# Two of four weight sums by accumulating DMA, and block pairs at the end of a feed-forward group

## The chip, the cores and the metric

The kernel runs on one core of a Trainium2 chip. The metric is the device time of one launch in microseconds; lower is better. TensorE (PE) does matmuls, VectorE (DVE), ScalarE (ACT) and GpSimd (POOL) do elementwise work, SyncE (SP) and GpSimd issue DMAs. Each engine takes its instructions in order, from its own queue.

## The reference

A two-layer encoder over 256 positions with a model width of 2048, in float32. Each layer does:

```
h = rmsnorm(x, norm1_g);  q, k, v, uv = h @ w_in
x = x + concat(rmsnorm(attention(q, k, v)), rmsnorm(gating(uv))) @ w_out
h = rmsnorm(x, norm2_g)
x = x + (silu(h @ w_gate) * (h @ w_up)) @ w_down
```

The change concerns the last two lines: the feed-forward part with w_gate and w_up (2048 x 5632 each), and what stands at its start.

## The kernel before

Every weight matmul is made in a 32-bit reduced type, with both operands split into a high part `hi` and a remainder `lo`; three terms (hi with hi, hi with lo, lo with hi) are summed in PSUM. `split` makes a weight's parts: ScalarE copies the raw weight to `hi` (L858), VectorE subtracts to get `lo` (L859). A raw weight tile, a `hi` and a `lo` of 128x2048 each lie in one of 17 buffers (`Big`, 1 MB). SyncE's queue issues the loads (L830).

The work is a list of groups: projections, out projections (`oa`, `og`), then 11 feed-forward groups a layer, with groups of the down projection between them. In the trace's names, group 9 is the first feed-forward group of layer 0 (here called group 0 of the layer), 10 the next, 11 the third. One feed-forward group makes 512 columns of gate and 512 of up, for both halves of the positions: four PSUM banks v, z (gate and up, first half) and x, w (second half). Its contraction of 2048 rows is eight pairs of 256 rows. Four pairs are done in the ordinary way ("N", two slots of 12 matmuls each: slot one into v and z, slot two into x and w). The other four, the block pairs, go through seven products M1 to M7 in place of eight (a 2x2 block product with seven multiplications), one slot of 12 matmuls each. So a group has 15 slots. The products need sums of weights, which `split` places by `add` (L836) on VectorE: T1 = q11 + q12 after M1's split, T2 = T1 + q22 after M5's (both in q11's buffer), T4 = q21 + T2 after M2's, T3 = q12 + q22 ahead of M3's. They also need sums of the normalized input `h`: `Norm.block` transposes a 512-column block of x (`tpn`), ScalarE scales it to `hr_n`, and `sums` makes seven forms (L252), their `hi` (L255, ACT) and `lo` (L256, DVE), together `h_n`. Ordinary pairs need only `hb_n`, a `hi` and a `lo`.

What sets the order is written by hand: `ORDER` is the order of slots of a group, `FIRST` that of a layer's group 0. Splits are placed two slots ahead of their use (three in group 0), loads five slots ahead; a list of events merges both. Side work (norm blocks, transposes of the feed-forward result `tpf` and its split `ff`) are generators that a scheduler steps through between slots. `finish` takes a bank's result out once its last matmul is done: banks 1 and 5 to 7 are the products' partial results, which it combines (`m1`, `m5`, `m16`, `m5_16`); with v complete `sil` (SiLU on ScalarE, L623) and with z the product with it (L626).

```
ORDER = ("N", "M1", "N", "M5", "M2", "N", "M6", "M3", "M7", "M4", "N")
FIRST = ("M1", "M5", "M2", "M6", "M3", "N", "M7", "N", "M4", "N", "N")
```

Of the kernel before, what the change touches and what calls it, by code (L numbers as in the profile page):

```python
# [14 lines left out]
P = 128  # L15
# [88 lines left out]
def encoder_kernel(ctx: ExitStack, tc: tile.TileContext, x, xf, w, ws, lng, cols, fg, cs, msk, out):  # L104
# [139 lines left out]
    def sums(raw, n, dst):  # L244

        r = raw.view("p (j f q) -> p j f q", j=2, f=8)[:, :n]
        f = lambda i: r[:, :, i, :]
        for to, a, op, b in (
            (3, f(7), ALU.subtract, f(2)), (4, f(3), ALU.subtract, f(0)),
            (5, f(0), ALU.subtract, f(7)), (6, f(1), ALU.add, f(4)),  # L250
        ):
            nc.vector.tensor_tensor(out=f(to), in0=a, in1=b, op=op)  # L252
        src = r[:, :, 0:7, :].rearrange("p j f q -> p j (f q)")
        hi, lo = (dst.rearrange("p (j h z) -> p j h z", h=2, z=7 * P)[:, :, i] for i in range(2))
        nc.scalar.activation(out=hi, in_=src, func=AF.Copy)  # L255
        nc.vector.tensor_tensor(out=lo, in0=src, in1=hi.bitcast(F32), op=ALU.subtract)  # L256
        raw.free()
# [16 lines left out]
    class Norm:  # L274


        def __init__(self, l, which, fast):
            self.l, self.which, self.fast = l, which, fast
            self.ss = smp.tile([P, NT, D // NB], F32, tag="ssn", name=f"ssn_{which}_{l}", bufs=2)
            self.hs = hpool.tile([P, 7 * 2 * KR * P], F32R, tag="h", name=f"h_{which}_{l}")  # L280
            self.pairs, self.bigs = [], []
            at, half = 0, 0
            for p in range(KD // 2):
                if p < fast:
# [4 lines left out]
                if at + 8 * P <= 56 * P:  # L289
# [26 lines left out]
        def block(self, b):  # L316

            fast = [p for p in (2 * b, 2 * b + 1) if p < self.fast]
            raw = Big(f"hr_{self.which}_{self.l}_{b}") if fast else None
            for j in range(2):  # L320
                p = 2 * b + j
                g = [gcol(self.l, self.which, 2 * p + i) for i in range(2)]
                ps = transposes(xt[b], 2 * j, f"tpn_{self.which}_{self.l}_{p}")
                yield 1
                if p < self.fast:
                    r = raw.view("p (j f q) -> p j f q", j=2, f=8)[:, j]
                    nc.scalar.activation(out=r[:, 0:8:7, :], in_=ps[:, 0], func=AF.Copy, scale=g[0])
                    nc.scalar.activation(out=r[:, 1:3, :], in_=ps[:, 1], func=AF.Copy, scale=g[1])
                else:
                    put_splits(self.pairs[p], 0, ps, g)  # L330
                    self.ready[p] = True
                yield 1
            if fast:
                sums(raw, len(fast), self.hs[:, fast[0] * 14 * P:(fast[-1] + 1) * 14 * P])
                for p in fast:
                    self.ready[p] = True
                yield 1
            self.square(b)
# [402 lines left out]
    def done(l, what, idx, t, n, ps):  # L741
# [11 lines left out]
        else:  # L753
# [8 lines left out]
            if what == "og" and t == NT - 1:  # L762
                spawn(norms["n2", l].block(b), delay=1 + n, rank=0)
            if what == last_part:
# [12 lines left out]
    class Group:  # L777


        def __init__(self, g, spec):  # L780
            self.g = g
            self.l, self.what, self.idx, _, self.n, self.fast, _ = spec
            self.banks, self.copies = {}, {}
            rest = iter(range(self.fast, self.n))
            self.slots = []
# [47 lines left out]
        def add(self, to, of):  # L833
            cols = self.fast * NB
            a, b = (self.raw[q].t[:, :cols] for q in (to, of))
            nc.vector.tensor_tensor(out=a, in0=a, in1=b, op=ALU.add)  # L836

        def need(self, key):
            return 1 if isinstance(key, tuple) else 2

        def split(self, key, pieces=1):
# [6 lines left out]
            else:  # L848
# [4 lines left out]
                hi, lo = (z.t[:, :cols] for z in own)  # L853
            if key == "M3":
                self.add("q12", "q22")
            for i in range(pieces):
# [6 lines left out]
            elif key == "M5":  # L863
                self.add("q11", "q22")
            elif key == "M2":
                self.add("q21", "q11")
            elif not (isinstance(key, tuple) and key[1] == 0):
                raw.free()

        def run(self, i):  # L870
# [38 lines left out]
        def finish(self, b):  # L909
            ps, c = self.banks[b][0], self.copies  # L910
            if b in "15":
                c[b] = sx(f"m{b}_{self.g}")
                nc.scalar.activation(out=c[b], in_=ps, func=AF.Copy)
                return
            if b == "6":
# [5 lines left out]
            if b == "7":  # L921
                nc.vector.tensor_tensor(out=c["x"], in0=ps, in1=c["x"], op=ALU.add)
                nc.vector.tensor_tensor(out=c["5"], in0=c["5"], in1=c["x"], op=ALU.subtract)
                c["v"], c["w"] = c["1"], c["5"]
                return
            if b in c:
                nc.vector.tensor_tensor(out=c[b], in0=ps, in1=c[b], op=ALU.add)
                ps = c[b]
            t, n = next(k for k, v in BANK.items() if v == b)
            done(self.l, self.what, self.idx, t, n, ps)  # L930

    groups = [Group(g, spec) for g, spec in enumerate(_groups())]
# [103 lines left out]
def _stream(np, weights):  # L1036

    parts = []
    for l, _, idx, row, pairs, fast, blocks in _groups():
        ab = [weights[name][l, row:row + pairs * 2 * P, c:c + NB].reshape(pairs, 2, P, NB) for name, c in blocks]  # L1040
        z = np.stack(ab, 2)
        rest = iter(z[fast:])
        for m in _order(idx, pairs, fast):
            if m == "N":
                parts.append(next(rest).transpose(2, 0, 1, 3).ravel())
            for q in LOADS.get(m, ()):
                parts.append(z[:fast, int(q[1]) - 1, int(q[2]) - 1].transpose(1, 0, 2).ravel())
    return np.concatenate(parts)
# [54 lines left out]
```

## Time and profile before

| | us |
|---|---|
| median of 3 runs | 2194.11 (2193.1 to 2195.26) |
| the profiled execution | 2191.83 |
| its span in the trace | 2190.0 |
| TensorE busy | 2098.2 (96%) |
| VectorE busy | 1619.8 (74%) |
| ScalarE busy | 1072.1 (49%) |
| GpSimd busy | 79.4 (4%) |

Busy shares are means over the span. Times are those of one core; a row of a timeline gives its start from the span's start, its length, the engine, the line and what it writes and reads, and in brackets how long its engine had been idle and what ended that. Matmul rows overlap, since matmuls are pipelined: their starts, not their lengths, tell how fast they follow each other. "PEclk" in a table of windows is the granted clock of TensorE as a share of its full speed.

### The profile page before, as it was taken

What the parts mean: (1) busy time and instruction counts of PE and PEld (TensorE: products, weight loads), DVE (VectorE), ACT (ScalarE), POOL (GpSimd) and SP (SyncE); (2) the same over time, 40 slices, a digit from 0 to 9 for tenths busy, and PEclk for the clock granted to TensorE, in tenths of its full rate; (3) what the DMA queues carried; (4) which work ended last, traced back from release to release, by engine and by line L of the source; (5) the groups of instructions that cost most, each with busy time, mean ns of one, the idle gap of its engine ahead of it and who ended that gap; (6) DMA issues with size and microseconds to landing.
All of it is one profiled execution on the core that took longest, in us unless ns stands there. A gap on an engine that the chain in (4) does not pass through costs nothing.

```text
span 2190.0 us, 23316 instructions
## 1 busy us (share of the span) xinstructions
PE 2098.2 (96%) x9432; PEld 1720.2 (79%) x9432; DVE 1619.8 (74%) x1432; ACT 1072.1 (49%) x1153; POOL 79.4 (4%) x64
## 2 busy tenths in 40 slices
PE   8999998999999999999999999989999999999997
PEld 7878886778777877877788788867787778778775
DVE  5677668795798589769665776588948976996794
ACT  6446536454355355435453555454544553554453
POOL 0220000000000000000002200000000000000000
PEclk9999998999999999999999999989999999999999
DMA  8444463455444545545544355544454454456452
GB/s 337 183 144 174 173 230 118 165 210 218 187 178 171 213 157 189 200 184 204 200 182 165 135 192 192 192 166 175 160 228 173 160 210 187 173 195 221 177 215 77
DMA packets 58797, 405.81 MB, mean 185 GB/s; under 512 B 6592, under 2 KB 6592, under 8 KB 10560
## 3 DMA queue, kind: packets, MB, share of 16 engines
q1 hardware_dynamic: 58688, 404.31, 49.7%
q8 instruction: 74, 1.21, 0.2%
q14 instruction: 35, 0.29, 0.0%
HBM read 402.19 MB, written 2.10 MB: 185 GB/s over the span
## 4 chain that ended last, share of the span: by engine, by line
PE 80%; DVE 11%; issue 6%; ACT 3%; DMA 0%; SPq 0%; DVEq 0%; POOLq 0%; POOL 0%; ACTq 0%
PE mm_z L880 18%; PE mm_x L880 18%; PE mm_v L880 16%; PE mm_w L880 16%; PE mm L880 8%; DVE lo_M L859 5%; DVE lo L859 2%; ACT hi_M L858 2%; DVE hl L859 1%; PE sp L449 1%; DVE raw_q L836 1%; DVE rb_k L419 0%; PE op L489 0%; PE tpn_n L264 0%; DVE ff L235 0%
## 5 line engine op out<-in xcount | busy, mean ns | idle before, releaser
L859 DVE TENSOR_TENSOR hl<-raw,hl 128x1024 fp32r<-128x1024 f32 (+1 forms) x402 | 479.3, 1240 | 74.4 <-ACT hl L858 72.7
L858 ACT ACTIVATE hl<-raw 128x1024 fp32r<-128x1024 f32 (+1 forms) x402 | 399.9, 1048 | 124.6 <-PE mm_w L880 83.4
L859 DVE TENSOR_TENSOR lo_M<-raw_q,hi_M 128x2048 fp32r<-128x2048 f32 x154 | 350.4, 2286 | 51.0 <-ACT hi_M L858 51.0
L858 ACT ACTIVATE hi_M<-raw_q 128x2048 fp32r<-128x2048 f32 x154 | 288.1, 1909 | 131.3 <-DVE raw_q L836 111.2
L880 PE MATMUL mm<-hi_M,h_n 128*128 128x512 f32 x704 | 236.5, 397 | 1.7 <-DVE h_n L256 1.7
L859 DVE TENSOR_TENSOR lo<-raw,hi 128x2048 fp32r<-128x2048 f32 x88 | 200.7, 2285 | 32.1 <-ACT hi L858 21.9
L836 DVE TENSOR_TENSOR raw_q<-raw_q,raw_q 128x2048 f32<-128x2048 f32 x88 | 201.6, 2290 | 2.3
L858 ACT ACTIVATE hi<-raw 128x2048 fp32r<-128x2048 f32 x88 | 167.6, 1908 | 49.9 <-PE mm_w L880 43.0
L880 PEld LDWEIGHTS mm<-hi_M,h_n 128*128 128x128 f32 x704 | 134.2, 191 | 30.2 <-DVE h_n L256 2.6
L880 PE MATMUL mm_v<-hl,ff 128*128 128x512 f32 x528 | 136.2, 392 | 2.7 <-ACT ff L234 2.7
L880 PE MATMUL mm<-lo_M,h_n 128*128 128x512 f32 x352 | 138.8, 394 | 0.0
L880 PE MATMUL mm_x<-hl,ff 128*128 128x512 f32 x528 | 135.1, 391 | 0.0
L880 PE MATMUL mm_z<-hl,ff 128*128 128x512 f32 x528 | 134.0, 389 | 0.0
L880 PE MATMUL mm_w<-hl,ff 128*128 128x512 f32 x528 | 134.0, 389 | 0.0
L880 PE MATMUL mm_v<-hi,hb_n 128*128 128x512 f32 x352 | 123.3, 391 | 0.0
L880 PE MATMUL mm_z<-hi,hb_n 128*128 128x512 f32 x352 | 122.9, 390 | 0.0
L880 PE MATMUL mm_w<-hi,hb_n 128*128 128x512 f32 x352 | 122.7, 389 | 0.0
L880 PE MATMUL mm_x<-hi,hb_n 128*128 128x512 f32 x352 | 122.6, 389 | 0.0
L880 PE MATMUL mm_v<-hl,h_n 128*128 128x512 f32 x420 | 112.8, 401 | 9.5 <-ACT hl L858 4.8
L880 PEld LDWEIGHTS mm_v<-hl,ff 128*128 128x128 f32 x528 | 98.1, 188 | 25.0 <-ACT ff L234 3.7
L880 PEld LDWEIGHTS mm_z<-hl,ff 128*128 128x128 f32 x528 | 99.1, 188 | 20.7
L880 PEld LDWEIGHTS mm_w<-hl,ff 128*128 128x128 f32 x528 | 99.1, 188 | 20.7
(205 smaller groups left out, 3324.2 us busy)
## 6 DMA issues: line engine op xcount, KB each, us to landing
raw<-in_w SPq DMA_DIRECT2D x287, 1024.0 KB, 4.8
raw_q<-in_w SPq DMA_DIRECT2D x88, 1024.0 KB, 6.6
xt<-in_x SPq DMA_DIRECT2D x4, 512.0 KB, 13.7
out<-xt SPq DMA_DIRECT2D x8, 256.0 KB, 3.1
xf<-in_xf SPq DMA_DIRECT2D x3, 512.0 KB, 10.0
raw<-in_w SPq DMA_DIRECT2D x4, 256.0 KB, 6.3
lw<-in_ws SPq DMA_DIRECT2D x2, 512.0 KB, 5.5
lw<-in_lng SPq DMA_DIRECT2D x2, 512.0 KB, 6.3
```

What stands on the lines that cost most here:

```text
L449: nc.tensor.matmul(sp[:, t, :], lhsT=q[:, a, i, t * P:(t + 1) * P], rhs=k[:, b, i, :], start=(n == 0), stop=(n == len(TERMS) - 1),)
L836: nc.vector.tensor_tensor(out=a, in0=a, in1=b, op=ALU.add)
L858: nc.scalar.activation(out=hi[:, sl], in_=src[:, sl], func=AF.Copy)
L859: nc.vector.tensor_tensor(out=lo[:, sl], in0=src[:, sl], in1=hi[:, sl].bitcast(F32), op=ALU.subtract)
L880: nc.tensor.matmul(bank[0], lhsT=lhsT, rhs=rhs, start=bank[1], stop=stop)
```

## The change

Four edits. First, T3 and T4 are made by an accumulating DMA on GpSimd's queue (`add_dma`: the destination's contents plus the source's), T3 right after M5's split and not ahead of M3's, T4 as before after M2's. There are 22 feed-forward groups, so 44 such transfers, of 1 MB each. Second, the block pairs are the last four of the eight, made from blocks 2 and 3 of x and no longer 0 and 1, and `FIRST` begins with three ordinary pairs. Third, `Norm.block` makes both transposes of a block together, and `sums` leaves a step between the `hi` and the `lo` of the forms; the blocks of the second out projection are spawned later. Fourth, `finish` writes v's result to a tile of its own, `c11`, and holds bank w back until x is done where w's ordinary pairs end before M7, as they do now in group 0.

```
@@ -55,7 +55,7 @@
 
 
 ORDER = ("N", "M1", "N", "M5", "M2", "N", "M6", "M3", "M7", "M4", "N")
-FIRST = ("M1", "M5", "M2", "M6", "M3", "N", "M7", "N", "M4", "N", "N")
+FIRST = ("N", "N", "N", "M1", "N", "M5", "M2", "M6", "M3", "M7", "M4")
 LOADS = {"M1": ("q11", "q12"), "M5": ("q22",), "M2": ("q21",)}
 
 CH = 4 * NB
...
@@ -253,6 +253,7 @@
         src = r[:, :, 0:7, :].rearrange("p j f q -> p j (f q)")
         hi, lo = (dst.rearrange("p (j h z) -> p j h z", h=2, z=7 * P)[:, :, i] for i in range(2))
         nc.scalar.activation(out=hi, in_=src, func=AF.Copy)
+        yield 1
         nc.vector.tensor_tensor(out=lo, in0=src, in1=hi.bitcast(F32), op=ALU.subtract)
         raw.free()
 
...
@@ -315,26 +316,25 @@
 
         def block(self, b):
 
-            fast = [p for p in (2 * b, 2 * b + 1) if p < self.fast]
+            fast = [p for p in (2 * b, 2 * b + 1) if p >= self.slow]
             raw = Big(f"hr_{self.which}_{self.l}_{b}") if fast else None
+            ps = [transposes(xt[b], 2 * j, f"tpn_{self.which}_{self.l}_{2 * b + j}") for j in range(2)]
+            yield 1
             for j in range(2):
                 p = 2 * b + j
                 g = [gcol(self.l, self.which, 2 * p + i) for i in range(2)]
-                ps = transposes(xt[b], 2 * j, f"tpn_{self.which}_{self.l}_{p}")
-                yield 1
-                if p < self.fast:
-                    r = raw.view("p (j f q) -> p j f q", j=2, f=8)[:, j]
-                    nc.scalar.activation(out=r[:, 0:8:7, :], in_=ps[:, 0], func=AF.Copy, scale=g[0])
-                    nc.scalar.activation(out=r[:, 1:3, :], in_=ps[:, 1], func=AF.Copy, scale=g[1])
+                if p >= self.slow:
+                    r = raw.view("p (j f q) -> p j f q", j=2, f=8)[:, j + len(fast) - 2]
+                    nc.scalar.activation(out=r[:, 0:8:7, :], in_=ps[j][:, 0], func=AF.Copy, scale=g[0])
+                    nc.scalar.activation(out=r[:, 1:3, :], in_=ps[j][:, 1], func=AF.Copy, scale=g[1])
                 else:
-                    put_splits(self.pairs[p], 0, ps, g)
+                    put_splits(self.pairs[p], 0, ps[j], g)
                     self.ready[p] = True
-                yield 1
             if fast:
-                sums(raw, len(fast), self.hs[:, fast[0] * 14 * P:(fast[-1] + 1) * 14 * P])
+                yield from sums(raw, len(fast), self.hs[:, (fast[0] - self.slow) * 14 * P:(fast[-1] + 1 - self.slow) * 14 * P])
                 for p in fast:
                     self.ready[p] = True
-                yield 1
+            yield 1
             self.square(b)
 
         def early(self, k, src):
...
@@ -760,7 +760,7 @@
             else:
                 nc.vector.tensor_tensor(out=xb, in0=ps, in1=xb, op=ALU.add)
             if what == "og" and t == NT - 1:
-                spawn(norms["n2", l].block(b), delay=1 + n, rank=0)
+                spawn(norms["n2", l].block(b), delay=1 + n + 2 * idx, rank=0)
             if what == last_part:
                 if l + 1 < DEPTH:
                     if t == NT - 1:
...
@@ -835,6 +836,10 @@
             a, b = (self.raw[q].t[:, :cols] for q in (to, of))
             nc.vector.tensor_tensor(out=a, in0=a, in1=b, op=ALU.add)
 
+        def add_dma(self, to, of):
+            cols = self.fast * NB
+            nc.gpsimd.dma_start(out=self.raw[to].t[:, :cols], in_=self.raw[of].t[:, :cols], accum_op=ALU.add)
+
         def need(self, key):
             return 1 if isinstance(key, tuple) else 2
 
...
@@ -851,8 +856,6 @@
                 src = raw.t[:, :cols]
                 own = [Big(f"{z}_{self.g}_{key}", F32R) for z in ("hi", "lo")]
                 hi, lo = (z.t[:, :cols] for z in own)
-            if key == "M3":
-                self.add("q12", "q22")
             for i in range(pieces):
                 sl = slice(i * cols // pieces, (i + 1) * cols // pieces)
                 nc.scalar.activation(out=hi[:, sl], in_=src[:, sl], func=AF.Copy)
...
@@ -862,8 +865,9 @@
                 self.add("q11", "q12")
             elif key == "M5":
                 self.add("q11", "q22")
+                self.add_dma("q12", "q22")
             elif key == "M2":
-                self.add("q21", "q11")
+                self.add_dma("q21", "q11")
             elif not (isinstance(key, tuple) and key[1] == 0):
                 raw.free()
 
...
@@ -911,6 +915,8 @@
             if b in "15":
                 c[b] = sx(f"m{b}_{self.g}")
                 nc.scalar.activation(out=c[b], in_=ps, func=AF.Copy)
+                if b == "1":
+                    c["v"] = c[b]
                 return
             if b == "6":
                 c["x"] = sx(f"m16_{self.g}")
...
@@ -921,13 +927,19 @@
             if b == "7":
                 nc.vector.tensor_tensor(out=c["x"], in0=ps, in1=c["x"], op=ALU.add)
                 nc.vector.tensor_tensor(out=c["5"], in0=c["5"], in1=c["x"], op=ALU.subtract)
-                c["v"], c["w"] = c["1"], c["5"]
+                c["w"] = c["5"]
+                return
+            if self.fast and b == "w" and "w" not in c:
+                self.held = True
                 return
             if b in c:
-                nc.vector.tensor_tensor(out=c[b], in0=ps, in1=c[b], op=ALU.add)
-                ps = c[b]
+                to = sx(f"c11_{self.g}") if b == "v" else c[b]
+                nc.vector.tensor_tensor(out=to, in0=ps, in1=c[b], op=ALU.add)
+                ps = to
             t, n = next(k for k, v in BANK.items() if v == b)
             done(self.l, self.what, self.idx, t, n, ps)
+            if b == "x" and self.held:
+                self.finish("w")
 
     groups = [Group(g, spec) for g, spec in enumerate(_groups())]
     slots, loads, first_slot = [], [], {}
```

Line numbers move by two to four: the split is at L861 (ACT) and L862 (DVE), `add` at L837, `add_dma` at L841, `finish` between L917 and L937.

On VectorE, in a steady group (11, layer 0), from M5's split on. Before; `raw_11_q21<-raw_11_q21,raw_11_q11` is T4, `lo_11_6` the third ordinary pair's `lo`:

```order
L859 TENSOR_TENSOR lo_11_M5_3317<-raw_11_q11_3202,hi_11_M5_3316 128x2048
L836 TENSOR_TENSOR raw_11_q11_3202<-raw_11_q11_3202,raw_11_q22_3258 128x2048
L859 TENSOR_TENSOR lo_11_M2_3335<-raw_11_q21_3279,hi_11_M2_3334 128x2048
L836 TENSOR_TENSOR raw_11_q21_3279<-raw_11_q21_3279,raw_11_q11_3202 128x2048
L235 TENSOR_TENSOR ff_0_1_3333<-tpf_0_1_0_3351,ff_0_1_3333 128x2x256
L859 TENSOR_TENSOR lo_11_6_3359<-raw_11_6_3299,hi_11_6_3358 128x2048
L235 TENSOR_TENSOR ff_0_1_3333<-tpf_0_1_2_3377,ff_0_1_3333 128x2x256
L859 TENSOR_TENSOR lo_11_M6_3397<-raw_11_q11_3202,hi_11_M6_3396 128x2048
```

Now, where the third ordinary pair is number 2:

```order
L862 TENSOR_TENSOR lo_11_M5_3319<-raw_11_q11_3203,hi_11_M5_3318 128x2048
L837 TENSOR_TENSOR raw_11_q11_3203<-raw_11_q11_3203,raw_11_q22_3260 128x2048
L862 TENSOR_TENSOR lo_11_M2_3338<-raw_11_q21_3281,hi_11_M2_3337 128x2048
L235 TENSOR_TENSOR ff_0_1_3336<-tpf_0_1_0_3354,ff_0_1_3336 128x2x256
L862 TENSOR_TENSOR lo_11_2_3362<-raw_11_2_3301,hi_11_2_3361 128x2048
L235 TENSOR_TENSOR ff_0_1_3336<-tpf_0_1_2_3380,ff_0_1_3336 128x2x256
L862 TENSOR_TENSOR lo_11_M6_3400<-raw_11_q11_3203,hi_11_M6_3399 128x2048
```

T4's row is gone (and T3's, which stood behind `lo_11_M6`), and the third pair's `lo` stands behind the `ff` directly.

On VectorE, where the block operands of a layer's group 0 (group 9) are made. Before, ahead of and beside M1's split:

```order
L252 TENSOR_TENSOR hr_n2_0_0_2483<-hr_n2_0_0_2483 128x2x128 x4
L256 TENSOR_TENSOR h_n2_0_2330<-hr_n2_0_0_2483,h_n2_0_2330 128x2x896
L859 TENSOR_TENSOR lo_9_M1_2592<-raw_9_q11_2538,hi_9_M1_2591 128x2048
L836 TENSOR_TENSOR raw_9_q11_2538<-raw_9_q11_2538,raw_9_q12_2540 128x2048
L252 TENSOR_TENSOR hr_n2_0_1_2513<-hr_n2_0_1_2513 128x2x128 x4
L256 TENSOR_TENSOR h_n2_0_2330<-hr_n2_0_1_2513,h_n2_0_2330 128x2x896
```

Now; `hr_n2_0_2` and `hr_n2_0_3` are blocks 2 and 3:

```order
L862 TENSOR_TENSOR lo_9_2_2664<-raw_9_2_2625,hi_9_2_2663 128x2048
L862 TENSOR_TENSOR lo_9_M1_2707<-raw_9_q11_2659,hi_9_M1_2706 128x2048
L837 TENSOR_TENSOR raw_9_q11_2659<-raw_9_q11_2659,raw_9_q12_2661 128x2048
L252 TENSOR_TENSOR hr_n2_0_2_2695<-hr_n2_0_2_2695 128x2x128 x4
L862 TENSOR_TENSOR lo_9_3_2746<-raw_9_3_2681,hi_9_3_2745 128x2048
L257 TENSOR_TENSOR h_n2_0_2330<-hr_n2_0_2_2695,h_n2_0_2330 128x2x896
L252 TENSOR_TENSOR hr_n2_0_3_2732<-hr_n2_0_3_2732 128x2x128 x4
L257 TENSOR_TENSOR h_n2_0_2330<-hr_n2_0_3_2732,h_n2_0_2330 128x2x896
L862 TENSOR_TENSOR lo_9_M5_2791<-raw_9_q11_2659,hi_9_M5_2790 128x2048
```

The forms of `h` have moved behind M1's split and T1, with the fourth ordinary pair's `lo` (`lo_9_3`) between the two steps of block 2.

On ScalarE, at the end of group 0. Before:

```order
L858 ACTIVATE hi_9_M4_2835<-raw_9_q21_2589 128x2048
L858 ACTIVATE hi_9_6_2856<-raw_9_6_2819 128x2048
L858 ACTIVATE hi_9_7_2886<-raw_9_7_2854 128x2048
L858 ACTIVATE hi_10_4_2932<-raw_10_4_2884 128x2048
L623 ACT_TABLE_LOAD
L623 ACTIVATE sil_0_0_0_2944<-m1_9_2679,rstd_n2_0_2816 128x512
L623 ACTIVATE sil_0_0_1_2961<-m16_9_2756,rstd_n2_0_2816 128x512
L858 ACTIVATE hi_10_M1_2973<-raw_10_q11_2914 128x2048
```

Now:

```order
L861 ACTIVATE hi_9_M3_2853<-raw_9_q22_2743 128x2048
L917 ACTIVATE m5_9_2870<-mm_9_5_2857 128x512
L861 ACTIVATE hi_9_M7_2874<-raw_9_q12_2661 128x2048
L623 ACT_TABLE_LOAD
L623 ACTIVATE sil_0_0_0_2893<-c11_9_2890,rstd_n2_0_2817 128x512
L861 ACTIVATE hi_9_M4_2895<-raw_9_q21_2771 128x2048
L861 ACTIVATE hi_10_0_2936<-raw_10_0_2872 128x2048
L623 ACTIVATE sil_0_0_1_2968<-m16_9_2912,rstd_n2_0_2817 128x512
L861 ACTIVATE hi_10_M1_2974<-raw_10_q11_2916 128x2048
```

The SiLU of the first half, which reads `c11`, has moved ahead of `hi` of M4, and its table load with it.

## Rows read from the trace of the kernel before

**Rows 1.** The page: busy time by engine, and the chain that ended last by engine.
```profile
PE 2098.2 (96%) x9432; PEld 1720.2 (79%) x9432; DVE 1619.8 (74%) x1432; ACT 1072.1 (49%) x1153; POOL 79.4 (4%) x64
...
PE 80%; DVE 11%; issue 6%; ACT 3%; DMA 0%; SPq 0%; DVEq 0%; POOLq 0%; POOL 0%; ACTq 0%
```

**Rows 2.** Waits of TensorE: us in total, times, longest.
```profile
PE mm_v L880 <- DVE lo L859: 38.8, 34, 1.6
```

**Rows 3.** Timeline of TensorE at two third pairs, first and last of 18.
```profile
468.87 0.39 PE L880 MATMUL mm_v<-hi,hb_n 128*128 128x512 f32 x1
470.78 0.50 PE L880 MATMUL mm_v<-lo,hb_n 128*128 128x512 f32 x1 [1.52 <-DVE lo L859]
...
2108.32 0.50 PE L880 MATMUL mm_v<-lo,hb_n 128*128 128x512 f32 x1 [1.56 <-DVE lo L859]
```

**Rows 4.** Timeline of VectorE in a steady group, and last of ScalarE.
```profile
617.89 2.29 DVE L859 TENSOR_TENSOR lo_M<-raw_q,hi_M 128x2048 fp32r<-128x2048 f32 x1
620.21 2.29 DVE L836 TENSOR_TENSOR raw_q<-raw_q,raw_q 128x2048 f32<-128x2048 f32 x1
622.42 0.68 DVE L235 TENSOR_TENSOR ff<-tpf,ff 128x512 fp32r<-128x512 f32 x1
623.02 2.28 DVE L859 TENSOR_TENSOR lo<-raw,hi 128x2048 fp32r<-128x2048 f32 x1
...
628.02 2.29 DVE L836 TENSOR_TENSOR raw_q<-raw_q,raw_q 128x2048 f32<-128x2048 f32 x1
...
618.15 1.91 ACT L858 ACTIVATE hi<-raw 128x2048 fp32r<-128x2048 f32 x1
```

**Rows 5.** Windows: length, busy by engine, PEclk, DMA share, GB/s; groups 0, 1, end of wait.
```profile
347.50:403.50 56.00, 45.78 (x197) 36.94 (x197) 44.32 (x37) 30.83 (x36) 2.66 (x1) 0.88 0.50 188
403.50:448.00 44.50, 42.38 (x190) 34.42 (x189) 41.52 (x28) 24.10 (x18) 0.00 (x0) 1.00 0.41 160
361.50:364.00 2.50, 2.50 (x8) 2.11 (x9) 2.50 (x2) 0.00 (x0) 0.00 (x0) 0.50 0.00 0
```

**Rows 6.** Timeline of TensorE in the first slots of group 0.
```profile
355.58 0.47 PE L264 MATMUL tpn_n<-ident,xt 128*128 128x128 f32 x1 [3.98 <-DVE xt L757]
361.43 0.90 PE L264 MATMUL tpn_n<-ident,xt 128*128 128x128 f32 x3 [5.37 <-DVE xt L757]
```

**Rows 7.** The chain that ended last: one slot, M4's, of that steady group.
```profile
639.07 2.72 PE mm_x L880 x12
```

**Rows 8.** The line of weight loads (L830): us from issue to landing.
```profile
DMA to landing us min/median/max: 4.6/4.9/15.1
```

**Rows 9.** Timelines of GpSimd and VectorE where they lie alone and side by side.
```profile
291.06 0.69 POOL L271 TENSOR_TENSOR rstd_g<-rstd_g,mhalf 128x2 f32<-128x2 f32 x1 [46.03 <-DVE rstd_g L270]
381.07 2.66 POOL L271 TENSOR_TENSOR rstd_n<-rstd_n,mhalf 128x2 f32<-128x2 f32 x1 [89.32 <-DVE rstd_n L270]
380.90 2.28 DVE L859 TENSOR_TENSOR lo_M<-raw_q,hi_M 128x2048 fp32r<-128x2048 f32 x1
...
332.27 2.36 DVE L859 TENSOR_TENSOR hl<-raw,hl 128x1024 fp32r<-128x1024 f32 x2 [4.28 <-ACT hl L858]
100.57 3.44 DVE L859 TENSOR_TENSOR hl<-raw,hl 128x1024 fp32r<-128x1024 f32 x2
100.79 2.14 POOL L421 TENSOR_TENSOR ra_k<-ra_k,rb_k 128x512 f32<-128x512 f32 x1 [0.43 <-DVE rb_k L419]
```

**Rows 10.** Timelines of VectorE and ScalarE: forms of h, table load, SiLU.
```profile
344.99 1.55 DVE L252 TENSOR_TENSOR hr_n<-hr_n 128x256 f32<-128x256 f32 x4
348.31 2.02 DVE L256 TENSOR_TENSOR h_n<-hr_n,h_n 128x1792 fp32r<-128x1792 f32 x1 [1.77 <-ACT h_n L255]
...
346.58 1.70 ACT L255 ACTIVATE h_n<-hr_n 128x1792 fp32r<-128x1792 f32 x1 [4.79 <-DVE hr_n L252]
...
400.40 1.28 ACT L623 ACT_TABLE_LOAD   x1 [13.81 <-DVE m L927]
401.70 0.72 ACT L623 ACTIVATE sil<-m,rstd_n 128x512 f32<-128x512 f32 x1
```

More of the change, by code (lines that the diff above doesn't have):

```diff
@@ L288, in __init__ @@
                     continue
-                if at + 8 * P <= 56 * P:
+                if not fast and at + 8 * P <= 56 * P:
                     v = self.hs[:, at:at + 8 * P]
@@ L316, in block @@
         def block(self, b):
-            fast = [p for p in (2 * b, 2 * b + 1) if p < self.fast]
+            fast = [p for p in (2 * b, 2 * b + 1) if p >= self.slow]
             raw = Big(f"hr_{self.which}_{self.l}_{b}") if fast else None
+            ps = [transposes(xt[b], 2 * j, f"tpn_{self.which}_{self.l}_{2 * b + j}") for j in range(2)]
+            yield 1
             for j in range(2):
@@ L322, in block @@
                 g = [gcol(self.l, self.which, 2 * p + i) for i in range(2)]
[L323 to L328, printed above, removed]
+                if p >= self.slow:
+                    r = raw.view("p (j f q) -> p j f q", j=2, f=8)[:, j + len(fast) - 2]
+                    nc.scalar.activation(out=r[:, 0:8:7, :], in_=ps[j][:, 0], func=AF.Copy, scale=g[0])
+                    nc.scalar.activation(out=r[:, 1:3, :], in_=ps[j][:, 1], func=AF.Copy, scale=g[1])
                 else:
-                    put_splits(self.pairs[p], 0, ps, g)
+                    put_splits(self.pairs[p], 0, ps[j], g)
                     self.ready[p] = True
-                yield 1
             if fast:
-                sums(raw, len(fast), self.hs[:, fast[0] * 14 * P:(fast[-1] + 1) * 14 * P])
+                yield from sums(raw, len(fast), self.hs[:, (fast[0] - self.slow) * 14 * P:(fast[-1] + 1 - self.slow) * 14 * P])
                 for p in fast:
                     self.ready[p] = True
-                yield 1
+            yield 1
             self.square(b)
@@ L762, in done @@
             if what == "og" and t == NT - 1:
-                spawn(norms["n2", l].block(b), delay=1 + n, rank=0)
+                spawn(norms["n2", l].block(b), delay=1 + n + 2 * idx, rank=0)
             if what == last_part:
@@ L783, in __init__ @@
             self.banks, self.copies = {}, {}
-            rest = iter(range(self.fast, self.n))
+            rest = iter(range(self.n - self.fast))
             self.slots = []
@@ L796, in __init__ @@
             self.raw, self.hl = {}, {}
+            self.held = False
         @staticmethod
@@ L864, in split @@
                 self.add("q11", "q22")
+                self.add_dma("q12", "q22")
             elif key == "M2":
-                self.add("q21", "q11")
+                self.add_dma("q21", "q11")
             elif not (isinstance(key, tuple) and key[1] == 0):
@@ L923, in finish @@
                 nc.vector.tensor_tensor(out=c["5"], in0=c["5"], in1=c["x"], op=ALU.subtract)
-                c["v"], c["w"] = c["1"], c["5"]
+                c["w"] = c["5"]
+                return
+            if self.fast and b == "w" and "w" not in c:
+                self.held = True
                 return
             if b in c:
-                nc.vector.tensor_tensor(out=c[b], in0=ps, in1=c[b], op=ALU.add)
-                ps = c[b]
+                to = sx(f"c11_{self.g}") if b == "v" else c[b]
+                nc.vector.tensor_tensor(out=to, in0=ps, in1=c[b], op=ALU.add)
+                ps = to
             t, n = next(k for k, v in BANK.items() if v == b)
             done(self.l, self.what, self.idx, t, n, ps)
+            if b == "x" and self.held:
+                self.finish("w")
     groups = [Group(g, spec) for g, spec in enumerate(_groups())]
@@ L946, in encoder_kernel, with early @@
                 splits.append((s, gr, key))
+    def early(gr):
+        return 0
     events = sorted(
-        [(s - LA_LOAD, 0, i) for i, (s, *_) in enumerate(loads) if i >= KD // KR]
-        + [(s - (2 if gr.fast and gr.idx else LA_SPLIT), 1, i) for i, (s, gr, _) in enumerate(splits)]
+        [(s - LA_LOAD - early(gr), 0, i) for i, (s, gr, *_) in enumerate(loads) if i >= KD // KR]
+        + [(s - (2 if gr.fast and gr.idx else LA_SPLIT) - early(gr), 1, i) for i, (s, gr, _) in enumerate(splits)]
     )
@@ L1041, in _stream @@
         z = np.stack(ab, 2)
-        rest = iter(z[fast:])
+        rest = iter(z[:pairs - fast])
         for m in _order(idx, pairs, fast):
```

18 lines of the change are left out of this document (11 added, 7 removed).

## The prediction

> **What bounds the kernel now.** I read the busy shares first: TensorE is busy for 96% of the span, VectorE for 74%, and the chain that ends last runs through TensorE for 80% [rows 1]. So the kernel is bound by matmuls, and a change that leaves their number alone can only win back TensorE's idle time. The table of waits says what that idle time is: the largest entry is a matmul of bank v that waits 34 times, 38.8 us in all, for VectorE's `lo` [rows 2].
>
> The timeline shows where. In a steady feed-forward group the third ordinary pair reaches TensorE before its `lo` is there, and TensorE stands for about 1.5 us [rows 3]. The reader should compare 468.87 and 470.78: neighbouring matmuls start 0.23 apart, these two 1.91. Such a wait, 1.50 to 1.56 long, stands once in each of groups 2 to 10 of either layer, 18 in all, the last one at 2108.32. On VectorE the cause is a queue: `lo` of M2 at 617.89, then the sum T4 at 620.21 (2.29 long), a short `ff` at 622.42, and only at 623.02 the pair's `lo`, whose `hi` ScalarE had made by 618.15 + 1.91 = 620.06 [rows 4]. Nothing of the pair was late but its place behind T4.
>
> The second place is the border from the out projection to the feed-forward part, once a layer. The first group there takes 56.0 us and the next 44.5, 100.5 together; TensorE waits 3.98 and 5.37 for `xt`, and runs at a granted clock of 0.50 at the end of this, the lower of its two levels [rows 5, 6]. Fifteen slots of 2.72 [rows 7] are 40.8; with transposes of 1.8 and the like about 84.5 would do for both groups.
>
> **The sums.** A steady group loses two VectorE additions, T4 behind M2 and T3 before M3. T3 ran at 628.02, and behind it the matmuls of the group run without a wait [rows 4, 7]; its removal is costed at nothing. T4 does not: with it gone the `ff` can follow `lo` of M2 directly, so the pair's `lo` starts and ends 622.42 - 620.21 = 2.21 earlier, at 623.09 and not 625.30 [rows 4]. TensorE asked for it about 1.56 before 625.36, at 623.8, so the wait vanishes with 0.7 to spare. The other wait of a group, at its second pair, has only T1 ahead of it, which stays; I leave it. The gain is 18 x 1.54 = 27.7 by the first and last wait. A resumed pipeline costs more than the idle figure: 1.91 - 0.23 is 0.16 above 1.52, and the first matmul takes 0.50, not 0.39. That 0.27 in 18 places is 4.9 more. Together **32.6**.
>
> The new cost is the transfer's time to land. M4 starts on TensorE at 639.07 [rows 7]; its `hi` (1.9) and `lo` (2.28) come before, so T4 must be there by about 633.3 to hurt nobody [rows 4, 7]. It can be issued when `hi` and `lo` of M2 have read q21, at 620.2. That leaves 13.1 us. T3's transfer is issued behind M5's split and has some 20. No accumulating transfer stands in the trace. From below, a 1 MB weight load lands in 4.6 to 4.9; from above, the slowest load, queued behind others, took 15.1 [rows 8]. Since the sum reads two operands and writes one, I take twice a median load, 9.8 (my estimate), so 3.3 us are over. What waits behind it: `hi` of M4 on ScalarE, hence everything ScalarE makes after that; and the buffers of q11 and q22, which come free only when the transfer has read them, some 5 us later than now, so that a load queued on SyncE for one of them starts later. Loads are issued five slots ahead, 13.6 us, and land in 4.9, so this is covered.
>
> **GpSimd beside VectorE.** GpSimd now issues transfers while VectorE is at a `lo`. Rows speak of this in both directions. A tiny GpSimd op took 0.69 at 291.06 and 2.66 at 381.07 with a `lo` beside it, which itself kept its 2.28; elsewhere two VectorE splits took 3.44 with a GpSimd op beside them against 2.36 alone, 1.08 more [rows 9]. So an interference between nothing and 1.08 on VectorE, or some 2 us on the issue, is to be allowed for each transfer; I take nothing on VectorE, since the nearest row in size, the tiny op, left the `lo` at 2.28, and 1.08 was lost beside an op on 128x512 elements.
>
> The Trainium skill, "SBUF — State Buffer", section "Who interferes with whom", speaks for this: a VectorE instruction with two SBUF inputs contends with a GpSimd instruction that reads SBUF, not with one that only writes there, and descriptor generation is inferred to need the write interface alone. By it the sums would cost VectorE nothing; by the row they would cost up to 1.08 each. No run here shows yet which holds beside an issue.
>
> **The first group of a layer.** It now starts with three ordinary pairs, so its first matmuls need only xt's blocks 0 and 1, and the waits of 3.98 and 5.37 go [rows 6]. But the block pairs' operands are then made inside the group. Let G be its first matmul. Three pairs are six slots, 16.3, and eight transposes among them 1.8: M1 is due at G+18.1. Block 2's transposes come at G+8.2; ScalarE's copies end at 10.3, the sums (1.55) at 11.9, their `hi` (1.70) at 13.6. The `hi` and `lo` of the fourth pair stand ahead: ScalarE to 15.5, VectorE to 17.8. Then `lo` of block 2 (2.02) to 19.8, block 3's sums to 21.4, its `hi` to 23.1, its `lo` to 25.1 [rows 10]. M1's last half runs after that and ends at 26.1, not 20.8: **5.3 lost**. VectorE is then continuously busy: `lo` of M5 ends at 28.7, T2 31.0, `lo` of M2 33.6, M6 35.9, M3 38.2, M7 40.5, the copy `c11` 41.2. On ScalarE `sil` waits for this copy and stands ahead of `hi` of M4; with a table load (1.28) and itself 0.72 it ends at 43.2, `hi` of M4 at 45.1, `lo` at 47.4, where M4 was due at 45.1: **2.1 lost** (the row shows the table load and `sil`, [rows 10]). T4's transfer, issued at 33.6, may take 9.6 here before it is the later one. Four short VectorE ops (2.8) then stand ahead of the next group's first `lo`, 2.4 late, and its next two `lo` are 1.7 and 1.9 late. Sum 13.4: the two groups take 84.5 + 13.4 = 97.9 and not 100.5, a gain of 2.6 a layer, **5.2** together. Bounds: if these delays overlap, up to 8 more a layer; if the clock falls again or a chain step is missed, 4 a layer lost: -8 to +16.
>
> **Sum.** Span 2190.0 - 32.6 - 5.2 = 2152.2; the profiled execution has 1.8 around it (2191.83), so 2154.0; the median of the runs is 2.3 above that execution: **2156.3**. Own range 2146 to 2170 (5.2 replaced by its bounds, and some of the 4.9 not returned).
>
> **Rivals.**
> - *The transfer is late.* One mechanism, in `hi` of M4: each us beyond 13.1 stalls 22 groups. From 13.1 + 37.8 / 22 = 14.8 us it eats the whole gain. The 15.1 of the slowest load lies there [rows 8]; for it speaks too that an accumulation reads what it writes, and that GpSimd's op was held 2 us by VectorE [rows 9]. At 17 us: 22 x 3.9 - 37.8 = +48, 2242. Against it: the transfer engines are 41% busy in a steady group [rows 5]. Chance 0.18, slower.
> - *VectorE is slowed by the issues.* The T4 issue falls beside the third pair's `lo`: 1.08 x 22 = 24 given back, about 2180; with T3's hurting as well, at most 2194. Chance 0.10.
> - *The wait does not vanish but halves*, because the `ff`, or `hi` behind a slower ScalarE, ends the wait in T4's place; 18 x 0.9 = 16 given back, 2172. The spare 0.7 is thin. Chance 0.10.
> - *The first group keeps up*: ScalarE and VectorE run ahead of my chain, since the loads of ordinary pairs are early; 7.7 a layer less, about 2141. Chance 0.10.
>
> **How the numbers follow.** My forecast has 0.52. A measurement here can tell about 0.2%, 4.4 us. 2138 to 2190 holds the forecast, the third and fourth rival and most of the second. Faster: 0.52 + 0.10 + 0.10 + 0.06 of the second rival = 0.78; same 0.04, its rest; slower 0.18.
>
> **What would show it.** Right: no wait of bank v at the third pair in groups 2 to 10, steady groups some 1.8 shorter (44.5 to 42.7), landing of the sums under 13 us, and the first two groups about 98 with waits of an M1 matmul for `h_n` and of M4 for `lo`. Wrong: waits of `hi` of M4 on GpSimd's transfer, a `lo` that lasts longer than 2.28 beside a sum's issue, a TensorE clock of 0.5 in the first group's middle.

## The result and the profile after

The changed kernel takes 2158.78 us (2158.12 to 2160.09, four runs), the kernel before 2193.61 beside it: a ratio of 0.9841, 95% interval 0.9824 to 0.9859. It is faster by 1.6%. The prediction was 2156.3. The medians lie 34.8 apart; the two profiled executions, from which the waits and the stages below are read, lie 31.7 apart in span.

First the page: the busy times, and the one new kind of DMA (size of one, median us from issue to landing).

```profile
PE 2100.5 (97%) x9432; PEld 1725.6 (80%) x9432; DVE 1525.8 (71%) x1388; ACT 1072.7 (50%) x1153; POOL 117.7 (5%) x108
...
raw_q<-raw_q POOLq DMA_DIRECT2D x44, 1024.0 KB, 7.8
```

Beside [rows 1] VectorE lost 94 us of work, and TensorE makes the same number of matmuls. Then the waits of TensorE:

```profile
PE mm_v L884 <- DVE lo L862: 15.7, 16, 2.2
PE mm_v L884 <- DVE lo_M L862: 5.8, 6, 1.0
PE mm L884 <- ACT h_n L255: 4.1, 2, 2.1
PE mm L884 <- DVE h_n L257: 4.1, 4, 1.1
```

The largest of [rows 2] fell from 34 waits to 16; waits for `h_n` in M1 are new, and those for `xt` are gone. The next view is VectorE's timeline in a steady group (20), which answers to [rows 4]:

```profile
806.23 2.29 DVE L837 TENSOR_TENSOR raw_q<-raw_q,raw_q 128x2048 f32<-128x2048 f32 x1
808.44 2.28 DVE L862 TENSOR_TENSOR lo_M<-raw_q,hi_M 128x2048 fp32r<-128x2048 f32 x1
810.65 0.68 DVE L235 TENSOR_TENSOR ff<-tpf,ff 128x512 fp32r<-128x512 f32 x1
811.25 2.28 DVE L862 TENSOR_TENSOR lo<-raw,hi 128x2048 fp32r<-128x2048 f32 x1
```

TensorE's timeline at that pair:

```profile
813.95 0.39 PE L884 MATMUL mm_v<-hi,hb_n 128*128 128x512 f32 x1
814.17 0.39 PE L884 MATMUL mm_v<-lo,hb_n 128*128 128x512 f32 x1
```

`lo` of M2 is followed by the `ff` and at once by the pair's `lo`, and the pair's second matmul starts 0.22 after its first, where [rows 3] had 1.91. Last the windows of the changed kernel (length, busy by engine, PEclk, DMA share, GB/s): the first two groups of layer 0, group 20, and three stretches in which the clock fell to 0.50, the lower of its two levels.

```profile
349.15:400.16 51.01, 46.43 (x197) 36.96 (x196) 36.73 (x31) 26.73 (x30) 4.64 (x3) 0.93 0.58 186
400.16:447.79 47.63, 44.03 (x190) 35.57 (x188) 41.62 (x30) 24.15 (x18) 1.71 (x2) 0.96 0.67 222
793.11:835.70 42.59, 42.04 (x189) 34.50 (x188) 37.05 (x25) 23.81 (x18) 1.72 (x2) 1.00 0.68 215
164.00:166.00 2.00, 2.00 (x6) 1.53 (x6) 1.10 (x4) 1.38 (x4) 0.00 (x0) 0.51 0.00 0
372.30:379.00 6.70, 5.86 (x13) 4.17 (x14) 5.52 (x3) 5.58 (x11) 0.00 (x0) 0.50 0.20 61
402.90:406.40 3.50, 3.50 (x9) 2.73 (x9) 3.09 (x5) 1.58 (x2) 0.00 (x0) 0.51 0.60 253
```

The kernel before in group 20, and where its clock was low in group 0:

```profile
801.70:846.20 44.50, 42.38 (x190) 34.42 (x188) 41.32 (x27) 23.78 (x18) 0.00 (x0) 1.00 0.47 182
352.40:366.10 13.70, 5.14 (x14) 3.99 (x15) 13.63 (x10) 5.04 (x4) 0.00 (x0) 0.50 0.05 11
```

Group 20 lasts 42.59, where it lasted 44.50 before. The span fell from 2190.0 to 2158.3, by 31.7. To see where, I took the first matmul of each group from both traces. The 18 steady groups together went from 797.4 to 766.7, 30.6 less. The first two groups of a layer, both layers together, went from 201.5 to 197.3, 4.2 less. Two groups in which no edit of the change lies, the gate projections of either layer, went from 108.8 to 112.0, 3.2 more: in layer 0 two waits of 0.97 and 1.26 stand at the same place in both traces, and behind them the clock stays at 1.00 before and drops to 0.51 after (the window from 164). The three make 31.6.

### The profile page after: what moved, and what is told of

It reads as the page before. It is cut to its first block, busy times and chain, and to the rows that moved or that the text cites. A ratio compares the mean times of both kernels' runs of the same rounds, so it can differ in the third digit from the quotient of the medians.

```text
span 2158.3 us, 23529 instructions
## 1 busy us (share of the span) xinstructions
PE 2100.5 (97%) x9432; PEld 1725.6 (80%) x9432; DVE 1525.8 (71%) x1388; ACT 1072.7 (50%) x1153; POOL 117.7 (5%) x108
## 3 DMA queue, kind: packets, MB, share of 16 engines
q0 software_dynamic: 6336, 46.14, 10.9%
## 4 chain that ended last, share of the span: by engine, by line
PE 50%; DVE 5%; issue 2%; ACT 2%; DMA 1%; DVEq 0%; POOLq 0%; POOL 0%; ACTq 0%
PE mm_v L884 12%; PE mm_z L884 11%; PE mm_x L884 11%; PE mm_w L884 10%; PE mm L884 5%; DVE lo_M L862 2%; DMA raw_q<-raw_q 1%; ACT hi_M L861 1%; DVE lo L862 1%; PE tpf L265 1%; DVE hl L862 0%; PE sp L449 0%; PE tpn_n L265 0%; DVE m L937 0%; PE op L489 0%
## 5 line engine op out<-in xcount | busy, mean ns | idle before, releaser
L862 DVE TENSOR_TENSOR hl<-raw,hl 128x1024 fp32r<-128x1024 f32 (+1 forms) x402 | 478.9, 1240 | 65.3 <-ACT hl L861 63.5
L861 ACT ACTIVATE hl<-raw 128x1024 fp32r<-128x1024 f32 (+1 forms) x402 | 399.6, 1048 | 129.2 <-PE mm_w L884 80.7
L862 DVE TENSOR_TENSOR lo_M<-raw_q,hi_M 128x2048 fp32r<-128x2048 f32 x154 | 348.8, 2287 | 77.3 <-ACT hi_M L861 72.5
L861 ACT ACTIVATE hi_M<-raw_q 128x2048 fp32r<-128x2048 f32 x154 | 287.3, 1910 | 108.2 <-DMA raw_q<-raw_q 82.6
L862 DVE TENSOR_TENSOR lo<-raw,hi 128x2048 fp32r<-128x2048 f32 x88 | 201.1, 2285 | 41.9 <-ACT hi L861 31.5
L861 ACT ACTIVATE hi<-raw 128x2048 fp32r<-128x2048 f32 x88 | 167.1, 1907 | 54.4 <-PE mm_w L884 43.0
L884 PEld LDWEIGHTS mm_x<-hl,ff 128*128 128x128 f32 x528 | 98.5, 188 | 20.1
```

Source lines behind the costliest of these rows:

```text
L861: nc.scalar.activation(out=hi[:, sl], in_=src[:, sl], func=AF.Copy)
L862: nc.vector.tensor_tensor(out=lo[:, sl], in0=src[:, sl], in1=hi[:, sl].bitcast(F32), op=ALU.subtract)
L884: nc.tensor.matmul(bank[0], lhsT=lhsT, rhs=rhs, start=bank[1], stop=stop)
```

## The experiments

All times are medians of the runs, beside the kernel before on the same chip. The stages come from the first matmuls of the groups in each profiled execution. "Gate" are the two gate groups; a time of some 110.4 or 112 there means that the clock fell in one layer or in both, some 1.6 each, as it did in the profiled executions of the change and of five of the eleven experiments. Differences under 3 us are therefore read from the stages.

| kernel | median | 18 steady groups | first two groups, both layers | gate |
|---|---|---|---|---|
| before | 2193.6 | 797.4 | 201.5 | 108.8 |
| the change | 2158.8 | 766.7 | 197.3 | 112.0 |
| e1 T4 by transfer only | 2154.8 | 767.1 | 193.6 | 108.8 |
| e2 T3 by transfer only | 2194.7 | 797.1 | 201.4 | 110.2 |
| e3 T4 later on VectorE | 2170.8 | 781.5 | 194.6 | 110.4 |
| e4 new order only | 2195.7 | 796.9 | 205.1 | 108.8 |
| e5 both by transfer, old order | 2155.0 | 766.6 | 193.4 | 108.8 |
| e6 e1, T1 later | 2152.6 | 761.0 | 198.1 | 110.3 |
| e7 e1, transfer issued later | 2248.8 | 848.3 | 207.3 | 108.8 |
| e8 the change, four pairs first | 2165.6 | 766.9 | 203.8 | 110.4 |
| e9 e6, but T1 as before in group 0 | 2147.8 | 761.0 | 192.8 | 108.8 |
| e10 T4 later on VectorE, T3 by transfer | 2153.2 | 763.6 | 193.5 | 111.8 |
| e11 e10, T1 later but in group 0 | 2147.7 | 760.5 | 193.0 | 108.8 |

Code shown is the part of the edit that matters; the method `add_dma` is that of the change.

My theory was that T4's place ahead of the third pair's `lo` makes the wait. The rival was that VectorE simply had too much to do.

**e1, T4 alone.** Edit to the kernel before:

```
             elif key == "M2":
-                self.add("q21", "q11")
+                self.add_dma("q21", "q11")
```

> Before, with T4 alone made by the accumulating transfer; T3 and the order stay. Theory (the gain is T4's place ahead of the third pair's lo): nearly the whole steady gain of the change stands, steady groups 42.6 to 43.3 and not 44.5, span about 2190 - 31 = 2159, time about 2163; nothing is won at a layer's first group. Rival (the gain comes from VectorE having less work at all, two additions of 2.29 in each group): half of it, about 2178.

Measured 2154.83, ratio 0.9822 (0.9807 to 0.9837): one edit of one line gives the whole gain of the change. The steady groups take 767.1, as in the change. The expectation erred on a layer's start: it gained 7.9 there. There too T4 had stood ahead of something: of x's updates, so that the second wait for `xt` fell from 5.37 [rows 6] to 3.04, and in the second group of the third pair's `lo`, so that this group lasts 43.3 and not 44.5.

**e2, T3 alone.**

```
             elif key == "M5":
                 self.add("q11", "q22")
+                self.add_dma("q12", "q22")
...
-            if key == "M3":
-                self.add("q12", "q22")
```

> Before, with T3 alone made by the accumulating transfer; T4 stays on VectorE. Theory: the third pair's wait of 1.5 stays in all 18 groups, steady groups 44.5, time within 4 us of before (2190 to 2198). Rival (less VectorE work in general): half of the gain, about 2178.

Measured 2194.72, ratio 1.0005 (0.9996 to 1.0015). The same 2.29 of VectorE work taken out at another place gains nothing while T4 stays where it is.

**e3, T4 kept on VectorE and moved.** The addition is put on a list and made after the next ordinary pair's split (ahead of the next product's, if that comes first):

```
             elif key == "M2":
-                self.add("q21", "q11")
+                self.late.append(("q21", "q11"))
...
+            if key not in PRODUCT:
+                self.flush()
```

> Before, with T4 still added by VectorE, but issued behind the third pair's lo and not ahead of it (in the first group of a layer its place is as before). No transfer is added. Theory: the wait goes as with the transfer, and no group is held by a late one, so steady groups take 42.6 each: 18 x 1.9 = 34 less and some 2 more in the second groups, span about 2154, time about 2158. Rival (less VectorE work): no gain, about 2194.

Measured 2170.79, ratio 0.9896 (0.988 to 0.9913): between the two theories. The third pair's wait is gone, but the steady groups gained 15.9, not 34. The view of waits shows the second pair's now as the largest, and the window of group 20 says why:

```profile
PE mm_v L891 <- DVE lo L868: 16.7, 14, 1.2
```

```profile
795.98:839.79 43.81, 42.52 (x189) 34.35 (x188) 41.15 (x28) 23.69 (x17) 0.00 (x0) 1.00 0.49 189
```

VectorE is busy for 41.15 of the group's 43.81. Moved back, T4 makes every later `lo` later. In the next group the second pair's wait grew from 0.55 to 1.19 (twelve groups, 7.6 us). M3's `lo` comes late too, with T4 and T3 both ahead of it: M3 and M7 lose 0.5 to 0.65 in each of the 18 groups, 10.2 us. Together these are the 17.9 that e3 lacks beside 33.8 (e10). So with every addition still on VectorE the place is worth 15.9, and the rest needs an addition less on VectorE.

**e4, the order alone.** The changed kernel with the `add`s of before in the places of before.

> The changed kernel with both sums back on VectorE at their old places: the new order alone. Theory: steady groups 44.5 again. At a layer's start the two sums add 4.6 us to the chain of VectorE between M5 and M4, of which some 2 to 4 reach TensorE, so that the gain of 2.1 a layer there is gone: span 2188 to 2200 with the 1.6 that the gate group's clock may cost. Rival (the order is what wins): at least 10 us faster than before, under 2183.

Measured 2195.65, ratio 1.0012 (1.0002 to 1.0021). Without the transfers the new order loses 3.6 at the layers' starts: M4 waits there 0.80 for `hi` and 1.83 for `lo`, beside the waits in M1.

**e5, the sums alone.** Both transfers, and the order of before (the edits of e1 and e2 together).

> Before, with T3 and T4 both made by accumulating transfers and nothing else changed: the change without its new order. Theory after the first four runs (T4 alone carries the gain, T3's transfer is neutral, the new order costs some 2 us in each layer's first two groups): as with T4 alone, 2153 to 2157, so 2 to 5 faster than the whole change. Rival (the new order earns what the prediction gave it, 5.2): slower than the change, 2162 or more.

Measured 2155.03, ratio 0.9823 (0.9808 to 0.9837), the same as e1. Against the change it has the same steady groups and first two groups shorter by 3.9. So the new order costs 3.9 when the sums are transfers, too; the gain at the layers' starts is the sums'. "New order" stands here for the second to fourth edit together; no run separates them.

**e6, T1 later.** On top of e1, T1 goes behind the second pair's `lo`, with the list of e3:

```
             if key == "M1":
-                self.add("q11", "q12")
+                self.late.append(("q11", "q12"))
```

> T4 by transfer in the old order, and T1 on VectorE issued behind the second pair's lo and not ahead of it. Theory (what stands ahead of a pair's lo on VectorE makes its wait): the wait of 0.55 to 1.3 at the second pair goes, in the 14 groups that have it, with 0.3 of restart each: 12 to 16 us less than T4 alone, time 2139 to 2144. Rival (VectorE is loaded to the point where a sum moved back only moves the wait to M5, whose lo then comes 2.3 later): no gain, 2153 to 2157.

Measured 2152.60, ratio 0.9811 (0.9795 to 0.9827). The steady groups gained 6, half of what the theory gave: the second pair's wait is gone, and a shorter one came at M2, whose `lo` now comes just too late. The first two groups lost 4.5: in group 0 no pair follows M1, so T1 was left until M5's split, behind the block operands, M5 and with it x's updates came later, and the first wait for `xt` grew from 4.0 to 7.08.

**e7, a dose of lateness.** On top of e1 the transfer is issued behind M6's split, and GpSimd first copies a column of M6's `lo`:

```
+                if key == "M6":
+                    nc.gpsimd.tensor_copy(out=tick, in_=lo[:, 0:1].bitcast(F32))
+                    self.add_dma("q21", "q11")
```

> T4 alone by transfer in the old order, but GpSimd first copies one element per partition of M6's lo, so that the transfer is issued some 5 us later. A dose for the price of lateness. Theory (M4's hi must have the sum at about 30.2 us into a steady group; each us beyond it delays the group by one): transfers land at 31 to 36, 1 to 6 late, and the steady groups take 43.5 to 48: time 2185 to 2225, no gain left. Rival (M4's wait is taken up by the slack before the next group): under 2170.

Measured 2248.84, ratio 1.0251 (1.0235 to 1.0266): slower by more than the theory's upper end. Here is ScalarE at M4's `hi` in group 20:

```profile
852.75 1.91 ACT L863 ACTIVATE hi_M<-raw_q 128x2048 fp32r<-128x2048 f32 x1 [7.43 <-DMA raw_q<-raw_q]
```

TensorE at M4:

```profile
854.72 0.50 PE L888 MATMUL mm_x<-hi_M,h_n 128*128 128x512 f32 x1 [2.08 <-ACT hi_M L863]
857.04 0.79 PE L888 MATMUL mm_x<-lo_M,h_n 128*128 128x512 f32 x1 [1.82 <-DVE lo_M L864]
```

And the windows around it:

```profile
848.00:852.00 4.00, 4.00 (x19) 3.32 (x18) 1.00 (x2) 0.00 (x0) 0.00 (x0) 1.00 0.97 233
852.00:856.00 4.00, 1.13 (x4) 0.38 (x2) 1.30 (x1) 3.25 (x2) 0.00 (x0) 1.00 1.01 426
856.00:862.00 6.00, 4.96 (x12) 3.90 (x13) 5.97 (x5) 2.27 (x2) 0.00 (x0) 0.51 1.02 430
```

In two groups (24 and 47) the sum landed 31.9 and 31.2 us after the group's start; they took 2.3 and 1.6 longer than in e1: the lateness beyond 30.2 (1.7 and 1.0) and some 0.6 of restart. In group 15 it landed at 33.9, 3.7 late; the clock stayed at 1.00, and the group took 3.7 more than the 42.59 of one whose sum is in time. In group 20 it landed at 35.3, 5.1 late, and the group took 8.0 longer: TensorE stands for 3.9, the clock is at 0.51 for the six us behind, some 3 more, and 0.7 is a longer wait of the second pair. So in this group, where the stall was followed by a lower clock, the lateness cost 1.6 times itself.

**e8, four pairs first.** `FIRST` of the changed kernel becomes N N N N M1 M5 M2 M6 M3 M7 M4.

> The changed kernel with a layer's first group beginning with all four ordinary pairs, then M1, M5, M2, M6, M3, M7, M4. Theory (VectorE's chain from the block operands to M4's lo sets the group's end, wherever M1 stands): M1's waits shrink from 4.0 to under 2, but the products behind it wait instead; time 2154 to 2160 as the change. Rival (M1's waits and the clock that falls behind them are what the group loses): 4 to 7 less a layer, 2145 to 2151.

Measured 2165.64, ratio 0.987 (0.9856 to 0.9885), slower than the change by 6.9 and outside of both expectations. M1's wait did shrink, to 1.98, but a third thing came:

```profile
375.54 0.73 PE L884 MATMUL mm<-hi_M,h_n 128*128 128x512 f32 x2 [1.98 <-DVE h_n L257]
382.69 0.79 PE L884 MATMUL mm<-hi_M,h_n 128*128 128x512 f32 x1 [5.95 <-ACT m L917]
```

and ScalarE's timeline there:

```profile
380.24 1.91 ACT L861 ACTIVATE hi_M<-raw_q 128x2048 fp32r<-128x2048 f32 x1 [1.57 <-DVE tot_n L314]
382.06 0.58 ACT L917 ACTIVATE m<-mm 128x512 f32<-128x512 f32 x1
```

With four banks held open by ordinary pairs, the next product needs the fifth, the one that M1 has just filled. It comes free with ScalarE's copy of M1's result (L917), which stands behind a `hi` that itself starts late: 5.95 of wait.

**e9, T1 later but not in group 0.** e6 with T1 in its old place where the group is a layer's first.

> T4 by transfer in the old order, T1 behind the second pair's lo in every group but a layer's first, where it stays in its old place. Theory (with T1 later everywhere the steady groups won 0.3 each, and the first group lost 2.3 to 2.9 because the block operands stood behind it): the first group takes 53.5 again and the steady groups 42.3, time 2146 to 2149. Rival (the first group's loss is not T1's): 2152.

Measured 2147.84, ratio 0.9793 (0.9778 to 0.9807), as the theory said: 192.8 for the first groups, with the steady ones of e6.

**e10, T4 moved and T3 by transfer.** The edits of e2 and e3 together.

> T4 on VectorE behind the third pair's lo, T3 by transfer, old order. T3 alone by transfer won nothing, and T4 moved alone won 23. Theory (with T4 moved, VectorE's remaining additions keep it late up to the next group's second pair, so that taking any 2.29 out of the group's second half wins the rest): steady groups 42.6 and not 43.8, time 2154 to 2158, and no group is held by a late transfer. Rival (T4 must leave the stretch up to the third pair and its successor altogether): 2168 to 2171.

Measured 2153.18, ratio 0.9818 (0.9802 to 0.9835), just below the theory's range. The window of group 20:

```profile
789.90:832.50 42.60, 42.05 (x190) 34.50 (x188) 39.07 (x26) 23.82 (x18) 0.86 (x1) 1.00 0.62 216
```

T3's transfer alone is worth nothing (e2), T4's new place alone 15.9 in the steady groups, both together 33.8. So the two are not halves that add up: the move is worth 15.9 with T3 on VectorE and 33.5 with T3 off it (e2 against e10). And 33.8 is more than the change's 30.6, since no transfer is late: T3's has the time.

**e11, e10 with T1 later.** T1 behind the second pair's `lo`, except in group 0.

> As the run before, with T1 too behind the second pair's lo except in a layer's first group. Theory: steady groups 42.3, 2 to 4 less than T4 by transfer with the same T1, since none is held by a late sum: 2144 to 2148. Rival (VectorE has no room for T4 and T1 together in its queue behind the pairs): 2152 or more.

Measured 2147.70, ratio 0.9794 (0.9779 to 0.9808), with e9 the fastest: 0.5% less than the change, and with one transfer a group in place of two.

## Why the prediction was right, point by point

**The third pair's wait** went in all 18 groups, as forecast. The term of 32.6 was measured at 30.6, and in it two errors partly cancel, which is luck. Where no transfer is late (e10) the same groups gain 33.8, 1.88 a wait and not 1.81. Six groups of the change took 3.1 back. One sentence was too simple: "Nothing of the pair was late but its place behind T4". By e3 a new place alone gives 15.9 of the 33.8; the rest needs an addition off VectorE, and T3 serves for that as well as T4 (e10, e1).

**The transfer's time.** I took 9.8. T4's landed in 7.2 to 12.9, median 10.4; T3's in 6.9 to 8.6, median 6.95. T4's spread goes with the weight loads beside it: in e1, group 24, with one load issued 2.6 behind it and one about to land, it took 7.9; in group 15, with one load issued 0.3 ahead and one 3.1 behind, in 13.2. No run moved the loads. e7 moved the transfer, and the spread went along: 6.9 in the four groups where the only load beside it was about to land, 8.8 to 10.9 in the groups where a load was issued about 1 behind it. The 13.1 us that I allowed were 0.9 too many: group 15 of e1, where T4 took 13.2, lasted 1.0 longer than a group with its sum in time, and group 43, with 12.9, 0.7 longer, so the bound is 12.2.

What I missed besides is that a late transfer costs again, one group later. ScalarE's queue in group 15 of the changed kernel, where the sum landed after 12.45:

```profile
629.12 1.92 ACT L861 ACTIVATE hi_M<-raw_q 128x2048 fp32r<-128x2048 f32 x1 [6.10 <-DMA raw_q<-raw_q]
630.94 3.70 ACT L861 ACTIVATE hi<-raw 128x2048 fp32r<-128x2048 f32 x2
```

and TensorE in the group behind:

```profile
651.31 0.50 PE L884 MATMUL mm_v<-lo,hb_n 128*128 128x512 f32 x1 [1.29 <-DVE lo L862]
```

M4's `hi` waits at the head of ScalarE's queue, and the next splits are pushed behind; the second pair of group 16 then waits 1.29, where the same group waits 0.56 in e10. Five of the 18 groups pay 0.2 to 0.7 for lateness of either kind, 2.9 together. A sixth (48) pays 0.35 behind a sum that landed early; why is open. The prediction named "everything ScalarE makes after that" and priced it at nothing.

This wait of `hi` of M4 for the transfer is one of the signs by which the prediction would be wrong, and it is there 19 times, 82.6 us in all. It tells little: in the kernel before, a `hi` waited on ScalarE 22 times, 111.2 us in all, for a sum of VectorE's. Two numbers of the rivals were off as well: with both issues hurting, the second comes to 2156.3 + 2 x 24 = 2204 and not 2194, and the share of 41% for the transfer engines is that of a layer's second group, where steady group 20 has 47%.

**GpSimd beside VectorE** cost nothing, as taken: VectorE's `lo` has a mean of 2.285 in both kernels; the 42 `lo` and `lo_M` of the changed kernel that run beside an issue have 2.285 too, the longest 2.293. An issue takes GpSimd 0.86. The rival of 1.08 an issue falls. e7 shows the other half beside it. GpSimd's copy of one column and its issue:

```profile
841.24 2.11 POOL L874 COPY tick<-lo_M 128x1 f32<-128x1 f32 x1 [42.48 <-DVE lo_M L864]
843.29 0.85 POOL L841 DMA_DIRECT2D raw_q<-raw_q  x1
```

VectorE at the time:

```profile
841.02 2.28 DVE L837 TENSOR_TENSOR raw_q<-raw_q,raw_q 128x2048 f32<-128x2048 f32 x1
843.23 4.48 DVE L864 TENSOR_TENSOR lo_M<-raw_q,hi_M 128x2048 fp32r<-128x2048 f32 x2
```

The copy, of one element a partition, ends when VectorE's addition ends, 2.11 later; the issue beside the next `lo` takes its 0.85. The Trainium skill, "SBUF — State Buffer", section "Who interferes with whom", tells the two apart in this way, the second by inference only; these rows agree with both.

**The first groups.** The sum was near, 4.2 for 5.2, but by luck: its cause was wrong. I gave the gain to the new order, which removes the waits for `xt`. They did go, but the order costs 3.6 by itself (e4) and 3.9 with the sums (e5 against the change); it is the sums' removal that earns 8.1 there. Of the delays that I worked out for group 0, M1's 5.3 was measured as three waits of 1.14, 2.06 and 0.84, together 4.0, but then the clock stood at 0.50 for 6.7 us, which is 3.4 more, and from 403 at 0.51 for another 3.4 us, 1.7 more; I had the clock in the bounds and not in the sum, and "a TensorE clock of 0.5 in the first group's middle" was a sign of being wrong that did come. M4's 2.1 was 0.54, the next pair's 2.4 was 2.17, and the two behind it, 1.7 and 1.9, were one of 1.43. By the clock the two orders do not differ: the kernel before had 13.7 us at 0.50 in its group 0 (the window from 352.4), but e5, with both sums gone from the old order, has 10.2 there, as many as the change in its two falls. The step that failed here is the comparison: I worked out the new order with fewer additions and set it against the old order with all of them.

**The gate groups** were not in the prediction: 3.2 of the profiled span. No edit of the change lies in them, and the same drop stands in the profiled executions of e2, e3, e6, e8 and e10, in either layer or both, behind the same two waits. What decides it is open.

## What to carry to other kernels

- When a change has two parts, work out each against the same state of the other. Here one line of it (T4) gave 2154.8, and a part that looked like the rest of the gain cost 3.9.
- An operation in front of a late one costs its place and its length. Moving it is free only if the engine has slack behind. With VectorE busy for 41 of 44 us the move alone gave 15.9 of 33.8, taking T3 off alone gave nothing, and both together gave all.
- A transfer in an operand's path is best given to the sum with the most time (T3, some 20 us), and the sum with little time moved on its own engine (e10, e11). A transfer's median says little beside its spread: 7.2 to 12.9 here.

## What the hardware showed that I had not expected

- An accumulating transfer of 1 MB between two on-chip tiles landed in 6.9 at best, 1.4 times a plain load's median of 4.9; T4's, beside weight loads, had a median of 10.4.
- A stall of 3.9 on TensorE (e7) was followed by 6 us at a clock of 0.51, so that 5.1 of lateness cost 8.0; behind the same waits of 0.97 and 1.26 in the gate group the clock fell in some profiled executions and not in others.
- GpSimd's one-column copy took 2.3 on average (e7, 22 of them) behind VectorE's two-operand instructions, while its issues took 0.87.
